# HGRN2 and stick-breaking attention block: FFN and gated embedding by Strassen's seven products on 1024-token groups

## Chip, cores and metric

The kernel runs on one core of a Trainium2 chip. The metric is the device time of one execution in microseconds; lower is better. The profile was taken of one execution of the same program.

## What is computed

One decoder layer on x of 2048 tokens x 1024 channels, float32 throughout:

```
u    = rmsnorm(x) @ w_in                      # 1024 -> 3584 columns: q, f, i, gate; q, k, v
o_hg = hgrn2(q, f, i)                         # 4 heads, 128x128 state, chunks of 64 tokens
o_hg = rmsnorm(o_hg) * silu(gate)
o_sb = rmsnorm(stick_breaking(q, k, v))       # 8 heads of 64, strictly causal
h    = x + rmsnorm(concat(o_hg, o_sb) @ w_out)
u    = rmsnorm(h)
y    = (silu(u @ w_gate) * (u @ w_up)) @ w_down     # 1024 -> 2 x 2816 -> 1024
h    = h + rmsnorm(y)
out  = h + sigmoid(h @ ple_gate) * (p @ ple_proj)   # p: 2048 x 256
```

A stick-breaking weight is a[t,s] = sigmoid(z[t,s]) times the product of (1 - sigmoid(z[t,j])) over s < j < t.

## The kernel before

The tokens are cut into four groups of 512 (`NG`, `GT`). Every float32 product is made of three TensorE matmuls on operands that are split into a rounded part hi and a rest lo: hi·hi, lo·hi, hi·lo (`mm3`, L200 to L203). A weight tile of 128x512 is loaded by SyncE into one of four buffers `wr` (L196), cast to `wh` on ScalarE (L187), and its rest `wl` is taken on GpSimd (L188). The split pairs have three buffers.

TensorE runs its instructions in program order. The order on the other engines is made by a scheduler when the program is built, and each engine then runs its own list strictly in order. `weave` (L48) writes the program order: after each slot of a main stream, such as four matmul groups of a projection, it lets side streams do a step. Four stages follow one another:

- The input projection `in_proj` of groups 0 to 3, in 56 slots each. Beside it run the recurrence `hgrn` of the group before and a share of the attention.
- An attention unit is one 128-query block against one 512-key chunk of one head: two score matmuls into `z` (L351), two sigmoids on ScalarE (`f` L359, `be` L361), a running product `pt` on VectorE by a scan (L365), the weight `a` = be·pt on VectorE (L367), four 128x128 transposes of `a` on TensorE (L378), a cast `ah` (L381), its rest `al` on VectorE (L383), and two value matmuls (L394, L395). Groups 0 to 3 have 32, 64, 96 and 128 units.
- Of the attention, the shares of groups 2 and 3 are spread at one rate over the rest of `in_proj(2)`, `in_proj(3)`, `out_proj(0)` and the FFN of group 0 (`late_share`, L728). The recurrence of group 3 also lies beside the FFN of group 0 (L773).
- Then each group has `out_proj` (192 matmuls; it ends with `post_mix`, which is norm, residual add and norm on whole 128x1024 rows, L605), transposes of h for the FFN (`make_u`) and for the embedding (`make_h2`), `ple`, and `ffn`. Streams of neighbouring groups are woven: while group g's `out_proj` runs, group g-1's transposes and embedding are stepped, so that one group's norms lie beside the other's matmuls.

The FFN of a group (`ffn`, L631) goes through 11 blocks of 256 columns. `up_block` has 8 weight tiles of 128 x (256 gate, 256 up columns) and 96 matmuls; the sigmoid (L644) and two products (L645, L646) follow, and the result is split into `hdh`, `hdl` for `down_block`, which takes four hidden tiles at a time and adds PSUM into `y` in SBUF (L666). u, h and the hidden tiles stay in SBUF. A group's FFN has 1056 + 528 matmuls, its gate 192.

Of the kernel before, what the change touches and what calls it, by code (L numbers as in the profile page):

```python
# [15 lines left out]
P = 128  # L16
# [66 lines left out]
def hybrid_block(  # L83
# [12 lines left out]
    # ---------------------------------------------------------------- scratch in DRAM  # L96
# [11 lines left out]
    hg_s = scratch("hg_s", (HH, P, GT))  # L108
    o_s = [[dram.tile([P, GT], F32, tag=f"o_s{g}_{i}", name=f"o_s{g}_{i}") for i in range(ND)] for g in range(NG)]
# [4 lines left out]
    def ctile(name, shape, dt=F32):  # L114
        return const.tile(list(shape), dt, tag=name, name=name)
# [3 lines left out]
    identb = ctile("identb", (P, P), BF16)  # L119
    make_identity(nc, identb)  # L120
    maskneg = ctile("maskneg", (P, P), BF16)
# [28 lines left out]
    masks = {h: ctile(f"mask{h}", (P, P), U8) for h in (0,) + LEVELS if h <= WIDE}  # L150
# [4 lines left out]
    # ---------------------------------------------------------------- pools  # L155
# [14 lines left out]
    wpool = ctx.enter_context(tc.tile_pool(name="wpool", bufs=1))  # L170
    side = ExitStack()
# [84 lines left out]
    # ---------------------------------------------------------------- input projection  # L256
# [68 lines left out]
    # ---------------------------------------------------------------- stick-breaking attention  # L325
    def attention():
# [18 lines left out]
        def weights_of(ch, tb):  # L345
# [21 lines left out]
            nc.vector.tensor_tensor(a[:, :n], be[:, :n], pt[:, o + 1:], op=ALU.mult)  # L367
# [59 lines left out]
    # ---------------------------------------------------------------- HGRN2  # L427
# [100 lines left out]
    # ---------------------------------------------------------------- output projection, FFN, PLE  # L528
    def tok(pool, tag):
        return [pool["p"].tile([P, D], F32, tag=tag, name=tag, bufs=TT) for _ in range(TT)]  # L530

    def gain_rows(src):
        gb = []
        for i in range(2):
            gb.append(tmp())
            nc.sync.dma_start(gb[i], src[:, i * 512:(i + 1) * 512].to_broadcast((P, 512)))
        return gb

    def scaled(dst, r, gb):
        for i in range(2):  # L540
            d = dst[:, i * 512:(i + 1) * 512]
            nc.vector.scalar_tensor_tensor(d, d, r, gb[i], op0=ALU.mult, op1=ALU.mult)
# [4 lines left out]
    def out_load(pool, g, res):  # L547
        ops = []
        acc = None
        for i in range(ND):  # L550
            raw = tmp()
            nc.sync.dma_start(raw, o_s[g][i])
            if i >= HH:
                hi, lo = operand(*pool["u"])
# [10 lines left out]
            else:  # L565
                ops.append(split(*pool["u"], raw))
        res["o"], res["oss"] = ops, acc

    def out_proj(pool, g, res):
        t0 = g * GT  # L570
        ops, acc = res["o"], res["oss"]
        r_hg, r_sb = [], []
        mix = tok(pool, "tok")
        for half in range(2):
            cs = slice(half * 512, (half + 1) * 512)
            for part in range(2):
# [24 lines left out]
                if half == 1 and part == 1:  # L601
                    post_mix(pool, g, res, mix)
                yield

    def post_mix(pool, g, res, mix):  # L605
        t0 = g * GT
        hs = tok(pool, "h")
        gb = gain_rows(attn_post_norm[0:1])
        for t in range(TT):
            nc.sync.dma_start(hs[t], x[t0 + t * P:t0 + (t + 1) * P, :])  # L610
        rs = [row_rstd(backp, mix[t], junk()) for t in range(TT)]
        for t in range(TT):
            scaled(mix[t], rs[t], gb)
            nc.vector.tensor_tensor(hs[t], hs[t], mix[t], op=ALU.add)
        rs = [row_rstd(backp, hs[t], junk()) for t in range(TT)]
        for t in range(TT):
            nc.vector.tensor_scalar(mix[t], hs[t], rs[t], None, op0=ALU.mult)
        res["h"], res["mix"] = hs, mix

    def make_u(pool, res, bank_of):  # L620
        res["u"] = []
# [213 lines left out]
```

## Time and profile before

| what | value |
|---|---|
| time, three runs | 3212.98, 3209.33, 3212.26 us; median 3212.26 |
| span of the profiled execution | 3207.7 us (the median is 4.6 above it) |
| input projections with attention and recurrence | 0 to 1011 us |
| `out_proj(0)` and the wait for its norms | 1011 to 1138 us |
| FFN of group 0 with the last attention | 1138 to 1691 us |
| groups 1 to 3, output projection to embedding | 1691 to 3208 us |
| DMA, share of 16 engines, and bytes | 41.1%, 400.70 MB |

Read a row "x896 | 1198.7, 1339" as 896 instructions, 1198.7 us busy in all, 1339 ns each on average. Where TensorE works without a gap, a matmul's own duration overlaps its neighbours', so its pace is found by dividing a stretch by its matmuls.

### The profile page before, as it was taken

The numbers are of one execution on the slowest core, as the hardware profiler recorded it, in microseconds if no ns is written. First come the engines' busy times: TensorE is split into PE (matmuls) and PEld (weight loads), VectorE is DVE, ScalarE is ACT, GpSimd is POOL, SyncE is SP. The second block draws the span as 40 slices with busy tenths as digits, with TensorE's granted clock in tenths as the row PEclk, the third lists the DMA queues.
The fourth block names the chain that finished last, engine by engine and source line by source line (L and its number), as shares of the span: only waits on it lengthen the run. The fifth ranks groups of instructions, "written<-read, shape, count | busy, mean of one in ns | idle before, by whom it ended". The sixth has DMA issues, their size and how long they took to land.

```text
span 3207.7 us, 44851 instructions
## 1 busy us (share of the span) xinstructions
PE 3124.3 (97%) x15328; PEld 2555.3 (80%) x15328; DVE 1774.9 (55%) x2492; ACT 1431.9 (45%) x2608; POOL 1494.0 (47%) x1254
## 2 busy tenths in 40 slices
PE   8999999999999799999999999999999998999999
PEld 6878878888888678888887888887888887888877
DVE  3356889888888888888866221226222226222142
ACT  4454565555456555555555332334333334332233
POOL 5444434443445423343346444556444556444453
PEclk9999999999999899999999999999999999999999
DMA  7666455545545233333343433332433333333333
GB/s 199 196 178 207 145 173 162 162 144 148 168 138 183 74 93 114 99 113 97 102 134 101 145 96 95 109 112 93 148 98 96 118 106 92 99 94 95 94 107 103
DMA packets 308420, 403.56 MB, mean 126 GB/s; under 512 B 35808, under 2 KB 177120, under 8 KB 308192
## 3 DMA queue, kind: packets, MB, share of 16 engines
q1 hardware_dynamic: 308192, 400.70, 41.1%
q8 instruction: 121, 1.98, 0.3%
q14 instruction: 107, 0.88, 0.1%
HBM read 341.85 MB, written 58.72 MB: 125 GB/s over the span
## 4 chain that ended last, share of the span: by engine, by line
PE 73%; DVE 6%; POOL 3%; issue 2%; ACT 1%; DMA 1%; SPq 0%; DVEq 0%; POOLq 0%; ACTq 0%
PE mm L201 16%; PE mm L203 15%; PE mm L202 15%; PE z L351 3%; PE tr L378 3%; PE av L201 2%; PE z L203 2%; PE z L201 2%; PE av L203 2%; PE av L202 2%; PE z L202 2%; DVE pt L365 2%; PE hg L449 2%; PE av L395 2%; POOL wl L188 1%
## 5 line engine op out<-in xcount | busy, mean ns | idle before, releaser
L188 POOL TENSOR_TENSOR wl<-wr,wh 128x512 fp32r<-128x512 f32 x896 | 1198.7, 1339 | 1415.0 <-ACT wh L187 1239.5
L187 ACT CAST wh<-wr 128x512 fp32r<-128x512 f32 x896 | 555.1, 620 | 1252.4 <-PE mm L202 422.5
L201 PE MATMUL mm<-uh,wh 128*128 128x512 f32 x1696 | 694.5, 410 | 5.3 <-DVE ea L321 4.6
L203 PE MATMUL mm<-uh,wl 128*128 128x512 f32 x1696 | 668.9, 394 | 1.0 <-POOL wl L188 0.9
L202 PE MATMUL mm<-ul,wh 128*128 128x512 f32 x1696 | 665.7, 393 | 0.0
L203 PEld LDWEIGHTS mm<-uh,wl 128*128 128x128 f32 x1696 | 318.6, 188 | 75.6 <-POOL wl L188 2.3
L201 PEld LDWEIGHTS mm<-uh,wh 128*128 128x128 f32 x1696 | 320.2, 189 | 68.9 <-DVE ea L321 5.6
L202 PEld LDWEIGHTS mm<-ul,wh 128*128 128x128 f32 x1696 | 320.3, 189 | 59.8
L365 DVE TENSOR_TENSOR_SCAN pt<-f,cy 128x513 f32<-128x513 f32 x192 | 294.5, 1534 | 69.1 <-ACT f L359 68.1
L645 DVE TENSOR_TENSOR tmp<-mm,tmp 128x512 f32<-128x512 f32 x67 | 45.4, 688 | 428.8 <-ACT tmp L644 428.6
L367 DVE TENSOR_TENSOR a<-be,pt 128x512 f32<-128x512 f32 (+2 forms) x320 | 256.7, 802 | 27.8 <-ACT ah L381 0.5
L381 ACT CAST ah<-tr 128x512 fp32r<-128x512 f32 (+1 forms) x320 | 167.1, 522 | 212.9 <-PE tr L378 209.7
L201 PE MATMUL mm<-wh,uh 128*128 128x512 f32 x616 | 255.0, 414 | 0.3 <-DVE ea L308 0.3
L202 PE MATMUL mm<-wl,uh 128*128 128x512 f32 x616 | 242.3, 393 | 8.0 <-POOL wl L188 8.0
L203 PE MATMUL mm<-wh,ul 128*128 128x512 f32 x616 | 243.0, 394 | 0.0
L365 DVE TENSOR_TENSOR_SCAN pt<-f 128x129 f32<-128x129 f32 (+3 forms) x128 | 163.4, 1277 | 124.6 <-ACT f L359 124.5
L383 DVE TENSOR_TENSOR al<-tr,ah 128x512 fp32r<-128x512 f32 (+1 forms) x320 | 192.4, 601 | 44.1 <-ACT ah L381 43.2
L359 ACT ACTIVATE f<-z 128x512 f32<-128x512 f32 (+2 forms) x320 | 170.0, 531 | 98.9 <-PE z L351 58.9
L201 PE MATMUL mm<-wh,hdh 128*128 128x512 f32 x520 | 209.0, 402 | 0.3 <-DVE tok L664 0.2
L203 PE MATMUL mm<-wh,hdl 128*128 128x512 f32 x520 | 205.3, 395 | 0.0
L202 PE MATMUL mm<-wl,hdh 128*128 128x512 f32 x520 | 205.0, 394 | 0.0
L351 PE MATMUL z<-kt,q 128*128 128x512 f32 (+3 forms) x640 | 183.7, 369 | 0.0
(252 smaller groups left out, 5157.2 us busy)
## 6 DMA issues: line engine op xcount, KB each, us to landing
wr<-in_w_gate_up_dram SPq DMA_DIRECT2D x704, 128.0 KB, 2.2
wr<-in_w_in_dram SPq DMA_DIRECT2D x224, 256.0 KB, 3.0
wr<-in_w_down_dram SPq DMA_DIRECT2D x176, 256.0 KB, 2.6
kt<-k_s SPq DMA_DIRECT2D x80, 256.0 KB, 3.0
vt<-v_s SPq DMA_DIRECT2D x80, 256.0 KB, 3.0
q<-q_s SPq DMA_DIRECT2D x128, 128.0 KB, 3.5
wr<-in_w_out_dram SPq DMA_DIRECT2D x64, 256.0 KB, 2.7
wr<-in_ple_gate_dram SPq DMA_DIRECT2D x64, 256.0 KB, 2.6
```

The source lines that it names most:

```text
L187: nc.scalar.copy(hi, src)
L188: (lo_engine or nc.gpsimd).tensor_tensor(lo, src, hi.bitcast(F32), op=ALU.subtract)
L201: nc.tensor.matmul(o, l[0], r[0], start=start, stop=False)
L202: nc.tensor.matmul(o, l[0], r[1], start=False, stop=False)
L203: nc.tensor.matmul(o, l[1], r[0], start=False, stop=stop)
L351: nc.tensor.matmul(z[:, :n], st["q"][i][:, tb * P:(tb + 1) * P], ch["k"][:, :n], start=i == 0, stop=i == 1 and not diag)
L359: nc.scalar.activation(f[:, o:GT], z[:, :n], AF.Sigmoid, scale=-0.125)
L365: nc.vector.tensor_tensor_scan(pt[:, o:][:, ::-1], fr, fr, init, op0=ALU.mult, op1=ALU.bypass)
L367: nc.vector.tensor_tensor(a[:, :n], be[:, :n], pt[:, o + 1:], op=ALU.mult)
L378: nc.tensor.transpose(tr[:, tb * P:(tb + 1) * P], ch["a"][tb][:, sb * P:(sb + 1) * P], ident)
L381: nc.scalar.copy(hi[:, lo_c:], tr[:, lo_c:])
L383: nc.vector.tensor_tensor(lo[:, lo_c:], tr[:, lo_c:], hi[:, lo_c:].bitcast(F32), op=ALU.subtract)
```

## The change

The FFN and the embedding's gate no longer work on a 512-token group but on 1024 tokens, as 2x2 blocks, by Strassen's seven products in Winograd's form: seven block products instead of eight, with sums and differences of blocks ahead of them (`t_side`, `s_side`) and sums of the results behind them (`chain`, the end of `gate_up`, `post_y`). Matmuls of 128x512 go from 10752 to 9864.

- `gate_up(grp)` goes through 11 blocks of 256 gate and 256 up columns. A block has seven products of 24 matmuls, in the order 1, 2, 6, 7, 5, 4, 3. The token side is combined and split once per group on VectorE. The weight side is combined for each block: eight sums and differences of 128x512 on VectorE (`e = nc.vector`), then 14 casts on ScalarE and 14 rests on GpSimd. The hidden tiles' own combinations are four GpSimd instructions per block, and seven tiles of each block go to DRAM.
- `down(grp)` takes two blocks at a time, loads hidden tiles back from DRAM (14 in an iteration), splits them with the rest on VectorE, combines weights on GpSimd, and adds each of 28 PSUM results into SBUF. In the last iteration the 28 results of both groups are finished row block by row block, with norm, residual and the store of h2 (`post_y`).
- `ple(grp)` combines h2 transposed on VectorE (`s_side`) and the gate's weights on GpSimd; `turn_h2` transposes h2 and sends it through DRAM.
- h, h2, u, the transposed h2, the transposed p and the hidden tiles go through DRAM scratch.
- The attention must be done before the FFN: its shares are 19 units in the rest of `in_proj(0)`, 13 + 37 beside `in_proj(1)`, 27 + 55 beside (2), 41 + 52 beside (3), and 81 units in the 48 slots of `out_proj(0)` to `(2)`; all 45 steps of `hgrn(3)` lie in the 16 slots of `out_proj(0)`. The weight product `a` goes from VectorE to GpSimd.
- Then, with nothing woven in, come `out_load(3)`, `make_u(2)`, `make_pt` of all four groups and `out_proj(3)`. `make_u(3)` is called in the first `gate_up` block after its third product, with the single bank `hg`; after it one half of the buffers is opened.

The core of the diff:

```diff
             a = att.tile([P, GT], F32, tag="a", name="a", bufs=8)
-            nc.vector.tensor_tensor(a[:, :n], be[:, :n], pt[:, o + 1:], op=ALU.mult)
+            nc.gpsimd.tensor_tensor(a[:, :n], be[:, :n], pt[:, o + 1:], op=ALU.mult)
...
+    def make_pt(g, tags):
+        for i in range(TT // 2):
+            raw = tmp().rearrange("p (t d) -> p t d", t=2)
+            nc.sync.dma_start(raw, p[r0:r0 + 2 * P, :].rearrange("(t p) d -> p t d", p=P))
+            ...
+            e = tmp()
+            nc.scalar.copy(e, b)
+            for c in range(PLE // P):
+                nc.sync.dma_start(pt_s[g][c][:, 2 * i * P:2 * (i + 1) * P], e[:, c * 2 * P:(c + 1) * 2 * P])
+    CHAIN = (1, 2, 6, 7, 5, 4, 3)
+    SLOTS = {"u": (12, 16), "w": (4, 4), "wr": (9, 0), "acc": (11, 18)}
+    def chain(prod, c, b, sides=(0, 0, 0, 1)):
+        if prod == 1:
+            c["u"] = acc(sides[0], "cu")
+            nc.scalar.copy(c["u"], b)
+        elif prod == 2:
+            c[1, 1] = acc(sides[1], "c11")
+            add(nc.vector, c[1, 1], b, c["u"])
+        elif prod == 6:
+            add(nc.vector, c["u"], b, c["u"])
+        ...
+    def gate_up(grp, hooks):
+        ts = t_side(lambda i, j, k: u_s[g0 + j][4 * i + k], ND // 2, "u", nc.vector, nc.vector)
+        for fb in range(DFF // 256):
+            for prod in CHAIN:
+                e = nc.vector
+                ...
+                elif prod == 6:
+                    a[2, 1], a[2, 2] = wload(1, 0), wload(1, 1)
+                    s1 = [acc(0, "s1") for _ in range(2)]
+                    for n in range(2):
+                        add(e, s1[n], a[2, 1][n], a[2, 2][n])
+                        sub(e, a[2, 1][n], a[1, 1][n], a[2, 1][n])
+                        sub(e, a[1, 1][n], s1[n], a[1, 1][n])
+                        sub(e, a[1, 2][n], a[1, 2][n], a[1, 1][n])
+                    w = a[1, 1]
+                else:
+                    w = {7: a[2, 1], 5: s1, 4: a[2, 2], 3: a[1, 2]}[prod]
+                ws = [pair_of(t, "w", prod, nc.gpsimd) for t in w]
+                for q in range(2):
+                    b = mm_bank()
+                    for k in range(ND // 2):
+                        mm3(b, st, tt[prod][k], k == 0, k == ND // 2 - 1)
+                    chain(prod, cs[q], b)
+                    ...
+    def down(grp):
+        for f0 in range(0, nfb, 2):
+            for prod in DOWN:
+                ...
+                hs = [pair_of(load(hid_s[grp][f0 + k, prod - 1]), "u", prod, nc.vector) for k in range(nk)]
+                ops[prod] = (hs, [pair_of(t, "w", prod, nc.gpsimd) for t in w])
+                if not last:
+                    for i in range(TT):
+                        down_product(accs, i, prod, ops[prod], nk)
+            if last:
+                for i in range(TT):
+                    for prod in DOWN:
+                        down_product(accs, i, prod, ops[prod], nk)
+                    post_y(grp, i, accs[i])
...
+    out_load(NG - 1, res[NG - 1])
+    Stream(make_u(NG - 2, res[NG - 2], ["tr", "hg"])).drain()
+    for g in range(NG):
+        make_pt(g, ["z", "av"])
+    Stream(out_proj(NG - 1, res[NG - 1])).drain()
+    gate_up(0, {(0, 6): swap})
+    down(0)
+    gate_up(1, {(3, 3): lambda: turn_h2(0), (5, 3): lambda: turn_h2(1)})
+    down(1)
+    ple(0, {7: lambda: turn_h2(2), 5: lambda: turn_h2(3)})
+    ple(1, {})
```

The list of VectorE before, in an FFN block of a later group; `mm`, `z`, `av`, `tr`, `hg` are PSUM banks, and an arrow points from the inputs to the output:

```order
L645 TENSOR_TENSOR tmp_23643<-mm_23487,tmp_23643 128x512
L645 TENSOR_TENSOR tmp_23651<-z_23488,tmp_23651 128x512
L646 TENSOR_TENSOR tmp_23643<-av_23489,tmp_23643 128x512
L646 TENSOR_TENSOR tmp_23651<-mm_23490,tmp_23651 128x512
L188 TENSOR_TENSOR hdl_23648<-tmp_23643,hdh_23647 128x512
```

The same list after, from product 2 to product 6 of a `gate_up` block (`wr` are raw weight tiles, `s1` a sum of two, `c11` and `cu` results in SBUF):

```order
L689 TENSOR_TENSOR c11_18229<-z_18216,cu_18187 128x512
L689 TENSOR_TENSOR c11_18244<-av_18231,cu_18202 128x512
L689 TENSOR_TENSOR s1_18254<-wr_18246,wr_18250 128x512
L689 TENSOR_TENSOR s1_18255<-wr_18248,wr_18252 128x512
L686 TENSOR_TENSOR wr_18246<-wr_18162,wr_18246 128x512
L686 TENSOR_TENSOR wr_18248<-wr_18164,wr_18248 128x512
L686 TENSOR_TENSOR wr_18162<-s1_18254,wr_18162 128x512
L686 TENSOR_TENSOR wr_18164<-s1_18255,wr_18164 128x512
L686 TENSOR_TENSOR wr_18204<-wr_18204,wr_18162 128x512
L686 TENSOR_TENSOR wr_18206<-wr_18206,wr_18164 128x512
L689 TENSOR_TENSOR cu_18187<-tr_18272,cu_18187 128x512
```

GpSimd after, in the same block: the first and second weight tile of product 6 are `wr_18162` and `wr_18164`; `wr_18246`, `s1_18254` and `wr_18250` are the first tiles of products 7, 5 and 4:

```order
L682 TENSOR_TENSOR wl_18265<-wr_18162,wh_18264 128x512
L682 TENSOR_TENSOR wl_18301<-wr_18246,wh_18300 128x512
L682 TENSOR_TENSOR wl_18339<-s1_18254,wh_18338 128x512
L682 TENSOR_TENSOR wl_18379<-wr_18250,wh_18378 128x512
L682 TENSOR_TENSOR wl_18269<-wr_18164,wh_18268 128x512
```

VectorE made no weights before. Now product 6's weights stand in its list behind the two evictions of product 2 (`c11`), and on GpSimd three tiles of later products stand between the two tiles of product 6.

The attention on VectorE before, with `pt`, `a`, the carry `cy` and `al` in turn:

```order
L365 SCALAR_TENSOR_TENSOR pt<-f_219 128x513
L367 TENSOR_TENSOR a<-be,pt 128x512
L371 COPY cy_10707<-pt 128x1
L383 TENSOR_TENSOR al<-tr,ah 128x512
L365 SCALAR_TENSOR_TENSOR pt<-f_217,cy_10550 128x513
L367 TENSOR_TENSOR a<-be,pt 128x512
```

GpSimd after, beside an input projection, where `qp` is the recurrence's and `wl` the projection's:

```order
L375 TENSOR_TENSOR a<-be,pt 128x512
L486 TENSOR_TENSOR qp<-qp,pd 128x128x2
L375 TENSOR_TENSOR a<-be,pt 128x512
L196 TENSOR_TENSOR wl<-wr,wh 128x512
L486 TENSOR_TENSOR qp<-qp,pd 128x64x4
L375 TENSOR_TENSOR a<-be,pt 128x512
L196 TENSOR_TENSOR wl<-wr,wh 128x512
```

The weight product has left VectorE's list and stands between the weights' rests on GpSimd.

TensorE before, at the start of the last group's output projection, behind the FFN's `down_block` of the group ahead:

```order
L201 MATMUL mm<-wh,hdh 128x512
L202 MATMUL mm<-wl,hdh 128x512
L203 MATMUL mm<-wh,hdl 128x512
L584 MATMUL hg<-ones_137,acc 128x1 x4
L201 MATMUL mm<-wh,uh 128x512
```

TensorE after, at the same place:

```order
L626 MATMUL hg<-ident,tok 128x128 x4
L640 MATMUL z<-ident,tmp 128x128 x4
L640 MATMUL av<-ident,tmp 128x128 x4
L640 MATMUL z<-ident,tmp 128x128 x4
L640 MATMUL av<-ident,tmp 128x128 x4
L640 MATMUL z<-ident,tmp 128x128 x4
L640 MATMUL av<-ident,tmp 128x128 x4
L640 MATMUL z<-ident,tmp 128x128 x4
L640 MATMUL av<-ident,tmp 128x128 x4
L583 MATMUL hg<-ones_162,acc 128x1 x4
L209 MATMUL av<-wh,uh 128x512
```

Between the matmuls of `out_proj(2)` and those of `out_proj(3)` now stand only transposes: eight rows of `tok`, the normalised h, of which the last is shown, and eight of `tmp`, which holds p. Before, FFN matmuls went right up to them.

More of the change, by code (lines that the diff above doesn't have):

```diff
@@ L741, in hybrid_block @@
         Stream(in_u(front, in_norm(front, 0), us[0], ["mm", "mm", "mm", "mm", "z", "av", "tr", "hg"])).drain()
+        before = 0
         for g in range(NG):
@@ L763, in hybrid_block @@
     h = Stream(hgrn(NG - 1))
[L764 to L773 removed]
+    out_load(0, res[0])
+    todo = before + LAG + 1
@@ new lines, in hybrid_block @@
+    for g in range(NG - 1):
+        op = Stream(out_proj(g, res[g]))
+        u = Stream(make_u(g - 1, res[g - 1], ["hg"])) if g else idle
+        n = todo // (NG - 1 - g)
+        todo -= n
+        hg_n = HG_STEPS if g == 0 else 0
+        weave(op, 6, att_part(share(n, 6, OP_SLOTS)), (h, hg_n // 2, 1))
+        weave(op, OP_SLOTS - 6, att_part(n - share(n, 6, OP_SLOTS)), (h, hg_n - hg_n // 2, 1), (u, ND if g else 0, 0))
+        out_load(g + 1, res[g + 1]) if g + 1 < NG - 1 else None
+        if g == 0:
+            h.drain()
+        op.drain()
```

498 lines of the change are left out of this document (318 added, 180 removed).

## The prediction

> **What bounds the kernel now.** First the page's busy row, then its chain, then a table of six stretches (us from to, length, then busy us and instructions of PE, PEld, DVE, ACT, POOL, and the clock).
>
> ```profile
> PE 3124.3 (97%) x15328; PEld 2555.3 (80%) x15328; DVE 1774.9 (55%) x2492; ACT 1431.9 (45%) x2608; POOL 1494.0 (47%) x1254
> ...
> PE 73%; DVE 6%; POOL 3%; issue 2%; ACT 1%; DMA 1%; SPq 0%; DVEq 0%; POOLq 0%; ACTq 0%
> ```
>
> ```profile
> 0.00:1011.00 1011.00, 979.40 (x5418) 813.13 (x5418) 734.68 (x1095) 535.10 (x1043) 458.66 (x419) 1.00 0.57 168
> 1011.00:1138.00 127.00, 106.09 (x556) 85.25 (x556) 110.50 (x171) 70.20 (x135) 50.16 (x47) 0.91 0.34 107
> 1138.00:1691.00 553.00, 548.26 (x2796) 448.74 (x2794) 453.16 (x626) 298.87 (x555) 213.05 (x167) 1.00 0.36 109
> 1691.00:2300.00 609.00, 599.99 (x2660) 484.62 (x2660) 213.48 (x261) 226.84 (x381) 327.60 (x269) 1.00 0.36 112
> 2300.00:2600.00 300.00, 300.00 (x1314) 246.83 (x1314) 71.52 (x96) 98.91 (x162) 150.24 (x116) 1.00 0.34 104
> 2600.00:3208.00 608.00, 590.52 (x2591) 476.77 (x2589) 191.51 (x245) 201.93 (x336) 294.25 (x238) 0.99 0.32 99
> ```
>
> TensorE is the bound nearly everywhere. From 2300 to 2600 us it never rests, so its pace is 300.00/1314 = 0.228 us per matmul. VectorE is loaded up to 1691 us (734.68 of 1011, 453.16 of 553) and nearly free after that (71.52 of 300). Dropping matmuls therefore pays only if TensorE stays the bound while VectorE and GpSimd get more work. For that the durations matter: of a group its mean, of a line min/median/max.
>
> ```profile
> L188 POOL TENSOR_TENSOR wl<-wr,wh 128x512 fp32r<-128x512 f32 x896 | 1198.7, 1339 | 1415.0 <-ACT wh L187 1239.5 <-PE z L351 36.8 <-PE mm L202 24.2
> L187 ACT CAST wh<-wr 128x512 fp32r<-128x512 f32 x896 | 555.1, 620 | 1252.4 <-PE mm L202 422.5 <-PE mm L203 306.2 <-PE z L202 172.9
> L188 DVE TENSOR_TENSOR hdl<-tmp,hdh 128x512 fp32r<-128x512 f32 x88 | 75.7, 891 | 3.6 <-ACT hdh L187 0.7
> ```
>
> ```profile
> L188 POOL TENSOR_TENSOR wl<-wr,wh x896: 1260/1292/2463, 17.4 to 3193.8; 128x512 fp32r<-128x512 f32 x180
> L188 DVE TENSOR_TENSOR hdl<-tmp,hdh x88: 669/679/1794, 1176.5 to 3080.5; 128x512 fp32r<-128x512 f32 x88
> L365 DVE TENSOR_TENSOR_SCAN pt<-f,cy x192: 1265/1299/2409, 336.3 to 1644.7; 128x513 f32<-128x513 f32 x192
> L367 DVE TENSOR_TENSOR a<-be,pt x320: 279/692/1821, 100.2 to 1646.1; 128x512 f32<-128x512 f32 x96, 128x128 f32<-128x128 f32 x32, 128x384 f32<-128x384 f32 x32
> L666 DVE TENSOR_TENSOR tok<-mm,tok x116: 658/692/693, 1361.5 to 3111.7; 128x512 f32<-128x512 f32 x116
> ```
>
> VectorE operations on two SBUF inputs, and GpSimd's, stretch up to about the sum of both (669 to 1794 ns; 1260 to 2463). The one that reads PSUM (L666) never exceeds 693. So those two kinds exclude one another: what counts is their **common sum**, at their shortest.
>
> The Trainium skill ("SBUF — State Buffer", section "SBUF: two separate sides") says the same of a shared port pair: it is an exclusive lock between a GpSimd operation and a VectorE operation with two SBUF inputs, held for the whole instruction. By that rule the sums below are floors, and the front cannot be bound by TensorE alone; the 669 to 1794 agrees.
>
> **The change part by part** (us of the profiled span).
>
> *Matmuls.* 10752 - 9864 = 888 fewer, 888 x 0.228 = **-202** if TensorE stays the bound.
>
> *Front: four input projections, out_proj(0) to (2), all of attention and recurrence.*
>
> ```profile
> 0.00:220.00 220.00, 201.34 (x939) 164.36 (x940) 86.62 (x127) 103.02 (x194) 99.92 (x113) 0.98 0.66 193
> ...
> 920.00:1011.00 91.00, 90.38 (x500) 74.85 (x497) 79.60 (x108) 55.34 (x107) 48.24 (x37) 1.00 0.50 155
> ```
>
> TensorE: 979.4 + 106.1, + 548.3 less FFN(0)'s 1584 x 0.228 = 361, + 2 x 192 x 0.228 = 88 for two output projections: 1361 busy. At before's pace, gaps included: 1691 - 361 + 88 = 1418. The common sum: GpSimd is busy 721.9 up to 1691, 632 with each instruction at the shortest of its shape. Less FFN(0)'s 132 weights x 1.26 = 166; plus `a`, which GpSimd does in 1.26 instead of 0.69 (median): 224 x 1.26 + some 66 for the 96 shorter ones = 348; plus out_proj(1), (2): 46 x 1.26 = 58. That makes 872. VectorE: 192 scans x 1.265 + some 107 for the 128 shorter, 350; other two-input ones some 105. Together 1327, of which 120 fall in the first 220 us, where no attention runs until late. How tightly can these lock together? Summed at their shortest over the records of 920 to 1011 they fill 82.4 of 91, 0.91, the densest stretch there is; from 370 to 1011 it is 0.80. I take 0.91: 220 + 1207/0.91 = **1545**. Bounds: 1361 (TensorE alone) and 220 + 1207/0.80 = 1729. `al` and the evictions read PSUM and lie beside it.
>
> *Ahead of out_proj(3).* Before, attention covered these norms, and yet this was seen (start, length, in brackets the idle time and its end):
>
> ```profile
> 1089.92 1.40 POOL L222 TENSOR_SCALAR rstd<-ss 128x1 f32<-128x1 f32 x1 [0.65 <-ACT junk L229]
> 1090.06 1.20 DVE L614 TENSOR_TENSOR h<-h,tok 128x1024 f32<-128x1024 f32 x1
> ...
> 1090.23 0.77 PE L394 MATMUL av<-ah,vt 128*128 128x512 f32 x1 [4.41 <-ACT junk L229]
> ```
>
> ```profile
> L542 DVE SCALAR_TENSOR_TENSOR tok<-tok,rstd,tmp 128x512 f32<-128x512 f32 x64 | 62.5, 1023 | 9.3 <-POOL rstd L224 9.0
> L617 DVE TENSOR_SCALAR tok<-h,rstd 128x1024 f32<-128x1024 f32 x16 | 23.7, 1483 | 6.7 <-POOL rstd L224 6.7
> L614 DVE TENSOR_TENSOR h<-h,tok 128x1024 f32<-128x1024 f32 x16 | 22.2, 1416 | 0.0
> L229 ACT ACTIVATE junk<-h 128x1024 bf16<-128x1024 f32 x16 | 16.9, 1056 | 25.0 <-DVE h L614 24.7 <-POOL rstd L222 0.3
> ```
>
> ```profile
> tmp<-o_s SPq DMA_DIRECT2D x32, 256.0 KB, 2.9
> ...
> tmp<-in_p_dram SPq DMA_DIRECT2D x8, 256.0 KB, 3.0
> ```
>
> `post_mix(2)`: VectorE 8 x 1.02 + 4 x 1.42 + 4 x 1.48 = 20, two rounds of squares before and between some 10: 30. `out_load(3)` with 8 and `make_pt` with 16 tiles share 3 `tmp`: loads of 2.9 and 3.0, a cast, a store of about as much, some 15 and 24; `make_u(2)` 10. All in a row 79; beside one another in part, I take 60. TensorE has 7 us of transposes there. Then 192 x 0.228 = 44: **104** (bounds 51 and 123).
>
> *gate_up, a regular block.* 168 x 0.228 = 38.3 of matmuls. Busy there: GpSimd 18 x 1.3 = 23, VectorE 30 instructions, 21; neither fills it, so only order can stall. After product 2's last matmul VectorE must do, in its list's order, the second `c11` eviction (0.69) and five sums (0.68 each); then a cast (0.62); then GpSimd five rests (1.29), since three of later products stand ahead of product 6's second tile: 11.2 us. Of product 6's 24 matmuls 17 still follow, 3.9; unstalled it would be 5.5: a **stall of 9.6**, with means for medians 10.6; I take 10. The floor is 0, if c11's eviction did not hold the sums. Queued behind those sums are product 6's own evictions, which nobody needs before product 7's end.
>
> ```profile
> 200.00:205.00 5.00, 5.00 (x16) 4.13 (x16) 1.92 (x4) 2.37 (x6) 2.97 (x5) 0.50 0.84 312
> ...
> 1092.00:1097.00 5.00, 4.23 (x15) 3.34 (x15) 4.68 (x9) 2.04 (x5) 4.92 (x2) 0.55 0.00 0
> 1097.00:1105.00 8.00, 2.83 (x22) 2.01 (x22) 7.29 (x11) 2.71 (x6) 4.12 (x7) 0.68 0.00 0
> 1105.00:1115.00 10.00, 8.30 (x40) 6.46 (x39) 9.57 (x20) 6.17 (x12) 2.23 (x3) 0.57 0.18 54
> ```
>
> After a pause of 4.41 us (above) the granted clock is 0.55 to 0.68. A 5 us stretch at 0.50 loses 2.5: the least that a row shows, and what I take per stall. So 20 blocks x (38.3 + 10 + 2.5) = 1016.
>
> The Trainium skill ("TensorE: Matmul & The Clock Gate", section "Part 1: The HAM clock gate") has half clock after an idle window of about 3.4 us, until some 3.4 us of sustained work: 1.7 per stall, 16 us less in the sum. That the drop follows such a pause agrees with 0.55 after 4.41; that it ends so soon does not, since it lasts to 1115.
>
> First blocks: VectorE splits and combines u there, 52 more instructions; 60 x 0.78 + 15 of evictions = 62, taken 64; in group 0 also `post_mix(3)` and `make_u(3)` through one bank (8 x 1.4 = 11), 88. `turn_h2` 2 x 7. Sum **1182** (bounds 877, no stall at all, and 1230).
>
> *down.* An iteration is 38.3 of matmuls; VectorE 28 x 0.69 + 14 x 0.78 = 30; common sum 22 x 1.26 + 14 x 0.67 = 37, so 41 with imperfect locking, five times. The last has 84 matmuls, 19; but VectorE does 28 evictions and 48 two-input instructions of `post_y`, 19 + 48 x 0.85 = 60, and with its ends 69; next in its list stand the sums of the following stage, so TensorE waits. 2 x (205 + 69) = **548** (bounds 421, 580).
>
> *ple.* 432 matmuls, 98.5 each. ple(0): 44 instructions of `s_side` (29 to 39) ahead of product 2's evictions, `turn_h2` 2 x 10: 150; ple(1) 127. **277** (bounds 197, 320). End: 5.
>
> Sum 1545 + 104 + 1182 + 548 + 277 + 5 = 3661, against 3207.7. The median of the runs is 4.6 above that span, so **3665**.
>
> **The rivals.**
> - *TensorE stays the bound (faster).* The weights' sums are ready before product 2 ends, as the 4 + 4 weight pairs would allow, and the front keeps before's pace: 1418 + 104 + 877 + 461 + 210 + 5 = 3075, time 3080. It decides at a stall of (3212 - 3080)/20 = 6.6 us per block, all else as here. For it: average loads of 21 and 23 in 38. Against it: the list's order, and the stretching already in the front. 0.08.
> - *The common sum does not bind the front.* `a` on GpSimd relieves VectorE, which was the dense engine (79.60 of 91); the two interleave well. Front 1418: 3538. For it: GpSimd's mean load of 872 in 1418. 0.24.
> - *The clock stays down longer.* In the three rows 1092 to 1115 it costs 5 x 0.45 + 8 x 0.32 + 10 x 0.43 = 9.1 instead of 2.5 per stall: 20 x 6.6 = +132, 3797. For it: these rows; against: few long gaps in the trace of before to judge by. 0.17.
>
> **How the numbers follow.** The forecast, with VectorE and GpSimd binding the front and a stall in each block, 0.50: 3665. The remaining 0.01 is no change. The range 3420 to 3880 takes in the second and third rival and most of the unknown costs (front -127, if at before's pace, or +184; blocks ±50); the lower end leaves out the first rival, and all upper bounds at once. A measurement of this kernel tells about 0.2% from no change. Faster by more than that 0.08, within it 0.01, slower 0.91.
>
> **What would show it.** Right: TensorE has a gap of 5 to 10 us ahead of the product 6 matmuls in every gate_up block, ended by GpSimd's `wl`; the clock falls behind it; the front ends near 1545 with VectorE and GpSimd busy and stretched; a pause of some 55 us ahead of out_proj(3); some 50 us of waiting at the end of each `down`. Wrong: blocks of 38 to 40 us, a front under 1430, or `post_y` hidden behind the next matmuls.

## The result, and the profile after

The changed kernel takes 3775.61 us (median of 4 runs, 3771.53 to 3780.8), against 3211.31 for the kernel before in the same comparison: a ratio of 1.176, 95% interval 1.1744 to 1.1777. The forecast was 3665, in a range of 3420 to 3880. The span of the profiled execution is 3769.7 us, where 3661 were summed up.

First the page of the changed kernel: busy times, two of its slice rows (40 equal slices of the span, in tenths; `PEclk` is the granted TensorE clock), and the chain. The last line is the clock row of the kernel before.

```profile
PE 3115.8 (83%) x14440; PEld 2482.3 (66%) x14440; DVE 2150.4 (57%) x3042; ACT 1520.9 (40%) x2852; POOL 2069.5 (55%) x1756
...
PE   8999999999987766666888889966878888992668
...
PEclk9999999999998887877988889987878889996789
...
PE 49%; DVE 14%; POOL 11%; issue 11%; DMA 10%; ACT 4%; SPq 1%; POOLq 0%; DVEq 0%; ACTq 0%
```

```profile
PEclk9999999999999899999999999999999999999999
```

TensorE has 888 instructions fewer (15328 to 14440), and yet its busy time hardly falls (3124.3 to 3115.8): the same matmuls run at a lower clock, as the clock rows show, with 8 and 7 in many slices from the thirteenth on where there was 9 before. Its share of the chain falls from 73% to 49%; VectorE, GpSimd, DMA and the time in which no wait is seen (`issue`, 2% to 11%) grow. What TensorE waited for stands in the list of its waits (total us, times, longest):

```profile
PE tr L209 <- ACT wh L681: 111.7, 22, 12.5
PE mm L209 <- ACT wh L681: 109.7, 3, 65.1
PE hg L583 <- POOL acc L564: 67.4, 2, 35.5
PE tr L211 <- POOL wl L682: 65.4, 43, 2.9
PE z L209 <- ACT wh L681: 33.0, 4, 28.0
```

The first and the fourth row are the 22 gate_up blocks: once per block a wait for a cast weight, twice for a rest. The others stand at places that come once or twice: the ends of `down` and of `ple`, and the starts of `out_proj(1)` and `(2)`.

The stages, from the first matmul of each to the first of the next (worked out from the records of the trace), against the terms of the prediction:

| stage | predicted | measured |
|---|---|---|
| front, to the last matmul of out_proj(2) | 1545 | 1564.5 |
| wait ahead of out_proj(3), and out_proj(3) | 60 + 44 | 83.1 + 45.7 |
| gate_up, two groups | 1182 | 1196 |
| of it a regular block (18 of them, mean) | 50.8 | 50.6 |
| down, two groups | 548 | 574 |
| ple and the end | 282 | 306 |

The differences add up to the 109 us between 3661 and 3769.7.

### The profile page after: what moved, and what is told of

Same layout as the page of the kernel before. It is cut to its first block, busy times and chain, and to the rows that moved or that the text cites. A ratio compares the mean times of both kernels' runs of the same rounds, so it can differ in the third digit from the quotient of the medians.

```text
span 3769.7 us, 45073 instructions
## 1 busy us (share of the span) xinstructions
PE 3115.8 (83%) x14440; PEld 2482.3 (66%) x14440; DVE 2150.4 (57%) x3042; ACT 1520.9 (40%) x2852; POOL 2069.5 (55%) x1756
## 4 chain that ended last, share of the span: by engine, by line
PE 49%; DVE 14%; POOL 11%; issue 11%; DMA 10%; ACT 4%; SPq 1%; POOLq 0%; DVEq 0%; ACTq 0%
PE mm L209 9%; PE mm L210 9%; PE mm L211 9%; POOL wl L682 5%; DMA wr<-hid_s 5%; PE tr L386 3%; PE z L359 3%; DVE pt L373 2%; PE hg L457 2%; DVE y L689 2%; POOL hs L686 2%; DVE ul L682 2%; PE av L403 2%; POOL wr L686 1%; PE tr L211 1%
## 5 line engine op out<-in xcount | busy, mean ns | idle before, releaser
L209 PE MATMUL mm<-uh,wh 128*128 128x512 f32 x1344 | 560.2, 417 | 52.3 <-ACT wh L681 44.6
L375 POOL TENSOR_TENSOR a<-be,pt 128x512 f32<-128x512 f32 (+2 forms) x320 | 315.9, 988 | 315.0 <-DVE pt L373 222.7
L209 PE MATMUL mm<-wh,uh 128*128 128x512 f32 x1008 | 422.8, 419 | 76.1 <-ACT wh L681 65.1
L210 PE MATMUL mm<-wl,uh 128*128 128x512 f32 x1008 | 404.2, 401 | 6.3 <-POOL wl L682 6.0
L211 PE MATMUL mm<-wh,ul 128*128 128x512 f32 x1008 | 403.5, 400 | 0.0
L682 DVE TENSOR_TENSOR ul<-wr,uh 128x512 fp32r<-128x512 f32 x274 | 238.1, 883 | 221.2 <-ACT uh L681 220.4
L681 ACT CAST uh<-wr 128x512 fp32r<-128x512 f32 x274 | 166.5, 619 | 369.7 <-DMA wr<-hid_s 246.0
L209 PEld LDWEIGHTS mm<-wh,uh 128*128 128x128 f32 x1008 | 194.9, 193 | 128.0 <-ACT wh L681 67.9
L210 PEld LDWEIGHTS mm<-wl,uh 128*128 128x128 f32 x1008 | 194.9, 193 | 45.4 <-POOL wl L682 9.1
L211 PEld LDWEIGHTS mm<-wh,ul 128*128 128x128 f32 x1008 | 193.9, 192 | 45.4
```

The costliest lines, as they stand in the source:

```text
L209: nc.tensor.matmul(o, l[0], r[0], start=start, stop=False)
L210: nc.tensor.matmul(o, l[0], r[1], start=False, stop=False)
L211: nc.tensor.matmul(o, l[1], r[0], start=False, stop=stop)
L375: nc.gpsimd.tensor_tensor(a[:, :n], be[:, :n], pt[:, o + 1:], op=ALU.mult)
L681: nc.scalar.copy(hi, src)
L682: lo_engine.tensor_tensor(lo, src, hi.bitcast(F32), op=ALU.subtract)
```

## The experiments

Each experiment but the last is one run. The changed kernel's own four runs lie 9 us apart, so a gain of 10 us or less is not read from the time alone but from the stages in the trace.

**The stall in a gate_up block.** A timeline of one block of the changed kernel (start, length, in brackets the idle time before and what ended it), from the last matmul of product 2 to the second weight tile of product 6:

```profile
1884.36 0.39 PE L211 MATMUL av<-uh,wl 128*128 128x512 f32 x1
1884.88 0.69 DVE L689 TENSOR_TENSOR c<-av,cu 128x512 f32<-128x512 f32 x1 [1.97 <-PE av L211]
1885.49 1.28 DVE L689 TENSOR_TENSOR s<-wr 128x512 f32<-128x512 f32 x2
1886.69 1.29 DVE L686 TENSOR_TENSOR wr<-wr 128x512 f32<-128x512 f32 x2
1887.89 1.29 DVE L686 TENSOR_TENSOR wr<-s,wr 128x512 f32<-128x512 f32 x2
1888.62 1.14 ACT L681 CAST wh<-wr 128x512 fp32r<-128x512 f32 x2 [8.71 <-DVE wr L686]
1889.29 0.80 PE L209 MATMUL tr<-uh,wh 128*128 128x512 f32 x1 [4.54 <-ACT wh L681]
1889.31 3.47 POOL L682 TENSOR_TENSOR wl<-wr,wh 128x512 fp32r<-128x512 f32 x2 [7.37 <-ACT wh L681]
...
1892.71 1.31 POOL L682 TENSOR_TENSOR wl<-s,wh 128x512 fp32r<-128x512 f32 x1
1893.96 3.73 POOL L682 TENSOR_TENSOR wl<-wr,wh 128x512 fp32r<-128x512 f32 x3
...
1896.52 0.80 PE L211 MATMUL tr<-uh,wl 128*128 128x512 f32 x1 [2.00 <-POOL wl L682]
```

It is the chain of the order: VectorE evicts `c` only when TensorE has finished product 2, then come the sums, the cast, and the rests on GpSimd. Nothing there is busy for long; each waits for the one before. The windows of the same block (from, to, length, busy of PE, PEld, DVE, ACT, POOL, clock) show what the clock makes of it:

```profile
1884.00:1889.00 5.00, 0.75 (x4) 0.28 (x2) 4.12 (x7) 0.39 (x1) 0.00 (x0) 0.85 0.00 0
1889.00:1895.00 6.00, 4.15 (x8) 2.34 (x8) 1.39 (x3) 3.88 (x8) 5.69 (x4) 0.50 0.25 74
1895.00:1900.00 5.00, 3.48 (x8) 2.84 (x9) 0.69 (x1) 0.00 (x0) 5.00 (x5) 0.50 0.59 157
1900.00:1903.00 3.00, 3.00 (x12) 2.39 (x12) 0.39 (x1) 1.20 (x2) 1.47 (x2) 0.82 0.37 120
1903.00:1924.00 21.00, 21.00 (x93) 16.97 (x92) 9.82 (x15) 4.21 (x8) 6.52 (x5) 1.00 0.16 51
```

Two kernels took the two causes apart. The first writes the loads and sums ahead of product 1, and with them the pairs of products 1 and 2 (`a[1, 2]` is overwritten by the sums):

```diff
                 if prod == 1:
-                    a[1, 1] = wload(0, 0)
+                    a[1, 1], a[1, 2] = wload(0, 0), wload(0, 1)
+                    a[2, 1], a[2, 2] = wload(1, 0), wload(1, 1)
                     w = a[1, 1]
-                elif prod == 2:
-                    a[1, 2] = wload(0, 1)
-                    w = a[1, 2]
-                elif prod == 6:
-                    a[2, 1], a[2, 2] = wload(1, 0), wload(1, 1)
+                    ws1 = [pair_of(t, "w", 1, nc.gpsimd) for t in a[1, 1]]
+                    ws2 = [pair_of(t, "w", 2, nc.gpsimd) for t in a[1, 2]]
                     s1 = [acc(0, "s1") for _ in range(2)]
                     for n in range(2):
...
+                elif prod == 2:
+                    w = a[1, 2]
+                elif prod == 6:
                     w = a[1, 1]
...
```

> The loads and the eight VectorE sums of a gate_up block are written ahead of product 1's matmuls instead of behind product 2, so in VectorE's list they come in the block before. Theory (the list's order makes the stall: sums behind the c11 evictions, then the rests): the pause ahead of product 6 goes, a regular block takes 38 to 40 us instead of 50.8, 20 blocks give -220 to -250, time 3525 to 3555, and the clock in these blocks returns to 1.00. Rival (GpSimd's or the weight tiles' throughput sets the block): blocks stay at 45 us or more, time above 3650.

It (e1) took 3549.42 us, 226 less than the changed kernel's median. A regular block takes 38.9 us instead of 50.6, and TensorE does not pause in it. A window of ten blocks' length (its last 6 us lie in `down`):

```profile
1794.00:2181.00 387.00, 387.00 (x1682) 315.43 (x1681) 233.29 (x303) 122.76 (x207) 257.51 (x188) 1.00 0.34 108
```

VectorE, GpSimd and the weight loads keep up with a TensorE that never rests, so their throughput was not the limit. The loads moved along with the sums, but in the timeline above the sums follow `c` without a gap, so they were not waiting for weights. The second kernel leaves the sums where they are and moves only the two rests of product 6:

```diff
-                ws = [pair_of(t, "w", prod, nc.gpsimd) for t in w]
+                ws = [pair_of(t, "w", prod, nc.vector if prod == 6 else nc.gpsimd) for t in w]
```

> Of the changed kernel only the two rests wl of product 6 go to VectorE, behind the sums; the sums stay where they are. Theory (both lists add to the stall): the wait for the second weight tile behind three rests of later products goes, 3 x 1.29 us, while the wait for c11 and the sums stays: 4 to 6 us less per block, time 3655 to 3695. Rival (only VectorE's list counts): within 20 us of 3775. Rival (only GpSimd's list counts): blocks near 40 us, time near 3550.

e2: 3699.15 us, 76 less; a block takes 47.3 us, 3.3 less, a little short of the expected 4 to 6. Pauses per block went from 7.6 to 5.2 us. The wait for the cast stays at 4.5 us; the two waits for a rest become one of 0.5 to 1.0. So both lists add to the stall, and VectorE's is the larger part.

**What sets the front.** The theory on record was the common sum of two-input VectorE operations and GpSimd.

```diff
-            nc.gpsimd.tensor_tensor(a[:, :n], be[:, :n], pt[:, o + 1:], op=ALU.mult)
+            nc.vector.tensor_tensor(a[:, :n], be[:, :n], pt[:, o + 1:], op=ALU.mult)
```

> The weight product a goes back to VectorE; nothing else. Theory (VectorE's two-input operations and GpSimd's exclude one another, their common sum sets the front): the sum falls by 320 x about 0.5 us, input projections 1 to 3 go from 918 to 830 to 870 us, where TensorE is the bound again, time 3690 to 3730. Rival (VectorE is the dense engine of the front, and a on GpSimd relieves it): VectorE gains some 220 us, the three stages take 950 us or more, time 3800 or more.

e3: 3803.27 us, 28 more. The rival's time came, but not its stage: the three input projections took 940 us instead of 918, where the theory had at most 870 and the rival at least 950. Their window and what TensorE waited for longest in it, in the changed kernel, then in this one:

```profile
195.00:1113.00 918.00, 885.43 (x5070) 734.69 (x5070) 701.79 (x1000) 535.50 (x1062) 607.30 (x546) 0.99 0.53 156
...
PE av L403 <- DVE al L391: 12.9, 14, 2.2
```

```profile
195.00:1135.00 940.00, 892.46 (x5072) 731.89 (x5072) 801.67 (x1225) 536.39 (x1063) 381.88 (x321) 1.00 0.51 153
...
PE av L403 <- DVE al L391: 41.4, 51, 2.4
```

GpSimd lost 225 us and VectorE gained only 100 (`a` takes 171 us there, while its other operations on two SBUF inputs went from 438 to 391), and still the stretch became longer. With each operation at the shortest of its shape, the common sum fell from some 830 of 918 to some 744 of 940: it cannot be what set the 918. TensorE can: it is busy in 885 of 918, and in 892 of 940 now. Of the 33 and 48 us left, 12.9 and 41.4 are waits for VectorE's `al`. The theory falls here, and the second rival of the prediction (the common sum does not bind) holds for the input projections; that VectorE is the denser engine shows in the sign and in the waits for `al`.

**The stretch of out_proj(0) to (2).** From 1113 to 1565 us no engine is full, and the clock is down:

```profile
1113.00:1565.00 452.00, 324.57 (x1676) 266.15 (x1674) 273.62 (x388) 212.22 (x400) 220.13 (x217) 0.83 0.34 109
1565.00:1648.00 83.00, 19.66 (x73) 13.80 (x74) 35.90 (x43) 34.43 (x59) 31.27 (x28) 0.51 0.73 247
```

Two of its pauses, 31.9 and 35.5 us, stand before the first matmul of out_proj(1) and (2), which needs `out_load`'s sum of squares (third row of the waits above). The first attempt put attention there:

```diff
         hg_n = HG_STEPS if g == 0 else 0
+        cover = 12 if g else 0
+        n -= cover
+        for _ in range(cover):
+            att_stream.step(2)
```

> In out_proj(1) and (2) 12 of the attention units are put ahead of the first instruction of the output projection, the 128x1 matmuls that wait for out_load; the number of units stays the same. Theory (the pauses of 31.9 and 35.5 us stand only because no other TensorE work is in program order before the waiting instruction): they fall under 15 us each, time 3715 to 3745. Rival (the attention of these stages is slow by itself, or waits for the same engines): what is gained there is lost later, time within 15 us of 3775.

e4: 3766.6 us, 9 less. The pauses went (none over 5 us is left there), but the stretch to the last matmul of out_proj(2) became only 12 us shorter, for 67 us of pauses: attention without projection matmuls between its units is slow. A window in the first of the two places, and what TensorE waited for from 1300 to 1500 us:

```profile
1316.00:1355.00 39.00, 26.48 (x80) 17.90 (x81) 33.05 (x42) 23.85 (x48) 24.61 (x25) 0.65 0.66 220
```

```profile
PE av L403 <- DVE al L391: 20.6, 12, 4.7
PE av L402 <- ACT ah L389: 7.0, 9, 2.7
```

The twelve units lie between the last matmul of out_proj(0) at 1321.7 us and the first of out_proj(1) at 1370.0: 48 us, 4 us each. VectorE is busy for 33.05 of the 39 us shown, 15.3 of them with `post_mix`. But when `post_mix` is done, at 1338.0, it still takes 3.5 us from one `al` to the next. The rival holds. The other kernels build on the one with early sums (3549.42 us). One went at the cause of the pause, the buffers and SyncE's list:

```diff
-        gb = gain_rows(attn_post_norm[0:1], tmp)
+        gb = gain
...
-            nc.sync.dma_start(hs[t], x[g * GT + t * P:g * GT + (t + 1) * P, :])
+            nc.scalar.dma_start(hs[t], x[g * GT + t * P:g * GT + (t + 1) * P, :])
...
-            nc.sync.dma_start(h_s[g][t * P:(t + 1) * P, :], hs[t])
+            nc.scalar.dma_start(h_s[g][t * P:(t + 1) * P, :], hs[t])
...
+    gain = gain_rows(attn_post_norm[0:1], lambda: backp.tile([P, 512], F32, tag="gb", name="gb", bufs=2))
```

(To make room, `UB` went from 10 to 9.)

> On top of the kernel with early sums (3549): the gain rows of post_mix are loaded once into buffers of their own, and its loads of x and stores of h are issued by ScalarE, so that out_load's loads come early in SyncE's list and find free tmp buffers. Theory (the pauses of 36 and 32 us at the starts of out_proj(1) and (2), and part of that ahead of (3), are out_load waiting behind post_mix for buffers and in the list): 10 to 18 us less at each, time 3500 to 3525. Rival (the attention units around it set the pace, as where they were used as cover): within 10 us of 3549.

g3: 3538.90 us, 10.5 less, but not there: the pauses are still 30.1 and 35.4 us, and 6.8 us of the gain lie in the stage of out_proj(0), 245.7 to 238.9. SyncE's list now has the eight loads one behind another, yet issuing them takes 19.29 us. The rows of squares (`junk`) use the same three buffers; the third load is issued when the last row is done, the others as buffers come free:

```profile
1323.19 19.29 SPq L552 DMA_DIRECT2D tmp<-o_s  x8
...
1334.59 1.14 ACT L195 CAST uh<-tmp 128x512 fp32r<-128x512 f32 x2 [4.37 <-DMA h_s<-h]
```

The second row shows a wait that the edit itself made. The first two tiles had landed at 1325.81 and 1328.42 us, some 10 us earlier than in the changed kernel (1338.01 and 1338.69), but ScalarE casts them at 1334.59: the loads of x that it now issues stand ahead in its list, and the last of them waits for a store of h to land. So g3 does not tell whether the buffers set the pause. `post_mix` and then `out_load` pass through them in turn; what the pause would be with more buffers, or with those loads on another queue, was not tried. The last one here shifted attention between the three stages:

```diff
-        n = todo // (NG - 1 - g)
+        n = todo // (NG - 1 - g) if g else todo // 2
```

> On top of the kernel with early sums (3549): of the 81 attention units beside out_proj(0) to (2), 40 instead of 27 go to out_proj(0) and 20 to 21 to each of the others. Theory (out_proj(0) is set by the serial chain of the recurrence, 45 steps in 16 slots, so attention there is free): its stage stays within 10 us of 246 and the other two fall by 30 to 42 in all, time 3507 to 3520. Rival (the attention units themselves set the pace of these stages): out_proj(0) grows by as much, time within 12 us of 3549.

f7: 3544.33 us, 5 less. out_proj(0) grew by 16.5 us for 13 units more, the other two fell by 13 and 10. The theory's 10 us in out_proj(0) were passed, and the time is the rival's, though the exchange was not quite even: in out_proj(0) a unit costs 1.3 us, elsewhere some 1.8.

**The wait ahead of out_proj(3).** The transposes of p moved to in_proj(0):

```diff
-            h = Stream(hgrn(g - 1)) if g else idle
+            h = Stream(hgrn(g - 1)) if g else Stream(make_pt(i, ["z", "av"]) for i in range(NG))
...
-            weave(main, KQV - HG_START, att_part(before - before * HG_START // KQV), (h, hg_a, 1))
+            weave(main, KQV - HG_START, att_part(before - before * HG_START // KQV), (h, hg_a if g else NG, 1))
...
-    for g in range(NG):
-        make_pt(g, ["z", "av"])
```

> On top of the kernel with early sums (3549): the transposes of p of all four groups (make_pt) move from ahead of out_proj(3) into in_proj(0). Theory (the wait ahead of out_proj(3) is a chain through the three tmp buffers, of which make_pt is the last 31 us): 25 to 35 us less, time 3515 to 3525. Rival (out_load(3) and make_u(2) end no earlier, make_pt lay beside them): within 10 us of 3549.

f5: 3549.49 us: no change, and yet both halves moved. The wait ahead of out_proj(3) fell by 29.3 us, as the theory had it, and in_proj(0) grew by 31.0. There TensorE stood before the second tile of each group until its load had landed (four waits, 21.9 us, the longest 11.2), and the clock in that stage fell from 1.00 to 0.94. A second kernel loads each tile one step ahead, and its steps lie further apart:

```diff
...
+        ahead = p_load(*todo[0])
+        yield
+        for n, (g, i) in enumerate(todo):
+            raw = ahead
+            if n + 1 < len(todo):
+                ahead = p_load(*todo[n + 1])
+            yield
...
```

> On top of the kernel with early sums (3549): make_pt in in_proj(0) as in f5, but each tile of p is loaded one step ahead of its transposes, and the steps lie further apart. Theory (in f5 in_proj(0) grew by 31 us because TensorE waited in order for each load of 3 us): in_proj(0) grows by less than 10 us, the 29 us ahead of out_proj(3) stay gained, time 3520 to 3532. Rival (the wait is for the copy and the store through the three tmp buffers): in_proj(0) again above 195 us, time above 3540.

g2: 3527.13 us, 22 less: in_proj(0) grew by 8.6 us only, the waits for p are gone, and the 29.3 stayed.

**The ends of down.** VectorE or the common sum?

```diff
                 hr = load(h_s[g][r0:r0 + P, j * 512:(j + 1) * 512])
-                add(nc.vector, y, y, hr)
+                add(nc.gpsimd, y, y, hr)
```

> On top of the kernel with early sums (3549): the last sum of post_y, y + h, 32 instructions per group, goes from VectorE to GpSimd. Theory (at the ends of down the two-input operations of VectorE and all of GpSimd's exclude one another, so the common sum counts): each move adds 1.26 - 0.67 = 0.6 us, 5 to 20 us more in all, time 3554 to 3570. Rival (VectorE's list alone is the bound there): 32 x 0.7 us less, time near 3527.

f6: 3555.90 us, 6.5 more. (The sums are 16 in each group, 32 in both, so that the theory's price is at most 32 x 0.6 = 19.) The last iterations of the two groups took 65.9 and 91.1 us instead of 60.4 and 84.6 (59.6 to 60.4 and 84.6 to 86.3 in the other kernels with early sums, g1 aside), with less work on VectorE. The second of them with early sums, and then with the sum on GpSimd:

```profile
3155.00:3240.00 85.00, 20.51 (x87) 15.73 (x85) 79.06 (x115) 26.47 (x58) 34.31 (x39) 0.64 0.59 199
```

```profile
3159.00:3250.00 91.00, 20.06 (x86) 15.38 (x84) 74.44 (x99) 25.66 (x58) 55.61 (x55) 0.63 0.56 186
...
DVE y L924 <- POOL rstd L232: 6.7, 2, 4.8
```

VectorE is no longer full (74.44 of 91), GpSimd neither, and it is slower: the rival falls. Two readings are left. With each operation at its shortest the common sum was 84 of 85 us before the sums moved and is 94 of 91 with them: it is full here, as it was not in the front, though it passes the window, so it is no strict floor. But the last row, VectorE's wait for GpSimd's `rstd`, was not there with early sums; it is 6.7 us in each of the two iterations, about what they grew by. On GpSimd `rstd` now stands between the sums that were moved there. f6 does not tell these two apart.

**ple.** Two attempts on its waits of 64 and 30 us. In the first the stores of the output are issued by ScalarE:

```diff
-                    nc.sync.dma_start(out[r0:r0 + P, j * 512:(j + 1) * 512], y)
+                    nc.scalar.dma_start(out[r0:r0 + P, j * 512:(j + 1) * 512], y)
```

> On top of the kernel with early sums (3549): the stores of out in ple are issued by ScalarE instead of SyncE. Theory (SyncE's list is in order, a store that waits for its sum holds back the loads behind it, and TensorE waits 28 us in ple(0) for them): ple falls by 20 to 35 us, time 3515 to 3530. Rival (the wait is for the operands' own chain or for VectorE): within 8 us of 3549.

f8: 3549.51 us: nothing. The timeline of the changed kernel ahead of ple(1) suggests why: the first weights of the gate are not loaded behind a store but behind all loads of the token side.

```profile
3628.34 17.86 SPq L671 DMA_DIRECT2D wr<-h2t_s  x14
...
3647.08 3.34 SPq L671 DMA_DIRECT2D wr<-in_ple_gate_dram  x5
...
3650.91 1.62 POOL L682 TENSOR_TENSOR wl<-wr,wh 128x512 fp32r<-128x512 f32 x1 [57.71 <-ACT wh L681]
```

So the second put the first product's weights ahead of the token side:

```diff
-        ss = s_side(lambda i, j, k: h2t_s[g0 + i][4 * j + k], ND // 2, "u", nc.vector, nc.vector)
...
         ws = t_side(blk, ND // 2, "w", nc.gpsimd, nc.gpsimd)
+        tt = next(ws)
+        ss = s_side(lambda i, j, k: h2t_s[g0 + i][4 * j + k], ND // 2, "u", nc.vector, nc.vector)
```

> On top of the kernel with early sums (3549): in ple the first product's weights are loaded and split ahead of the token side, whose 28 loads and 44 VectorE instructions stand ahead of them in the lists. Theory (TensorE's waits of 64 us before ple(0) and 30 us before ple(1) are for the first weight tile, whose load is issued behind all token loads): together 20 to 50 us less, time 3500 to 3530. Rival (product 1's token pairs, behind post_y on VectorE, come as late): within 8 us of 3549.

g1: 3546.19 us, 3 less. What TensorE waited for (the second row lies in ple(1), the others in ple(0)):

```profile
PE mm L209 <- ACT uh L681: 39.7, 2, 39.4
PE mm L209 <- ACT wh L681: 16.1, 1, 16.1
PE tr L209 <- ACT wh L681: 13.5, 1, 13.5
```

The named waits did shrink, 64 to 39 us and 30 to 3; but from their first matmul on the two stages grew by 22 and 25. The wait of 39 is now for a token operand (`uh`), and those of 13.5 and 16.1 us stand ahead of product 2, whose weights are loaded behind the token side, as product 1's were. The wait moved on to the next weights in the same list.

**Together.** e1, g2, g3 and f7 in one kernel:

> Early sums, p early with loads ahead (g2), loads of post_mix apart (g3) and more attention in out_proj(0) (f7), together. If the gains lie in different pauses they add: 3549 - 22 - 11 - 5 = 3511, and the ratio to the kernel before is about 1.095, so still slower. If g3 and f7 gain in the same stage (out_proj(0)), 3516 to 3520. In neither case does it reach the kernel before; what then stands between them is the end of the two down stages, the first gate_up blocks, ple and the output projections of groups 0 to 2.

3518.42 us, ratio 1.0962 to the kernel before, interval 1.0944 to 1.098. The parts gave 31 of the 38 us that they had each shown, as expected if g3 and f7 gain in the same place: out_proj(0) took 259.8 us, where f7 alone had 262.2. No version that was run beats the kernel before.

## Why the prediction came out as it did

- *Matmuls.* -202 us was right as a count, and the full pace returns where nothing stalls (387 us for ten blocks, 1.00).
- *gate_up* was right in mechanism and place, shown by e1 (the whole stall goes) and e2 (a part). That 50.8 was predicted and 50.6 measured is partly luck, since its two terms were off against one another. The pauses are 7.6 us per block instead of 10, and the lower clock costs 50.6 - 38.7 - 7.6 = 4.3 instead of 2.5. That the slower matmuls of product 6 fill part of the wait for the second tile was left out. The sign that was named, one gap of 5 to 10 us ended by GpSimd's `wl`, came as three: 4.5 us ended by ScalarE's cast, then 1.1 and 2.0 for `wl`. Two blocks with `turn_h2` took 13 to 15 us more, where 7 was put.
- *Front.* 1545 against 1564.5 looks right and is not. The step that failed is "VectorE and GpSimd binding the front", a common sum at 0.91. e3 showed that the input projections are set by TensorE, with waits for VectorE's `al`. That the sum counted there and divided by 0.91 gives 912 us, where 918 were measured, is luck. In out_proj(0) to (2) it gives 363 (331 at the shortest), and 452 were measured, with TensorE's 1676 instructions busy for 325 even at a clock of 0.83. The sum itself was too large: the trace has some 1280 up to 1565 us instead of 1327, mostly because `a` takes 1.09 us on GpSimd at 128x512 and not 1.26. Nor did the sums as floors show that TensorE could not bind the front: 1327 is less than the prediction's own 1361 for TensorE. The two pauses of 67 us together were not on the list at all: the prediction looked for `post_mix` and `out_load` only where nothing is woven in, and took the attention as cover ahead of out_proj(1) and (2). In program order it stands behind the instruction that waits. What sets the rest of this stretch stays open: e4, g3 and f7 shortened it by 6 to 12 us only.
- *Ahead of out_proj(3).* The pieces, all in a row, had been put at 79 and were taken as 60; measured 83.1. They stand in a row: f5 took make_pt out, and the wait fell by 29, close to the 24 worked out for it, so it had not lain beside the rest. That the three `tmp` buffers are the reason was not tried.
- *down.* Regular iterations took 41 to 45, 42.8 on average, against 41; the last ones 59.9 and 86.0 against 69 each. VectorE is full in these (79.06 of 85), and f6 showed that its load alone does not decide. The second is longer because ple(0)'s token side follows in the same list, which was counted under ple: with the weights ahead of it (g1) this iteration took 60.4 to ple's first matmul.
- *ple.* 306 with the end, against 282: the token side's loads, ahead of the weights in SyncE's list, were missing. g1 showed that it is this list, not the first weight alone, that TensorE waits for.
- The rival of a clock that stays down longer (9.1 us per stall) did not come: 4.3. The rows from 1092 to 1115 us that it was worked out from hold more than one pause (TensorE busy in 2.83 of 8 us), so their 9.1 was not the price of one stall. The rival on the faster side needed a stall under 6.6 us per block; e1 made it 0, and 3549 instead of 3080 came, because its other condition, a front at before's pace with everything else unstalled, failed.

Where the 202 us of saved matmuls went, and 562 more: 226 to the blocks' stalls (e1). The other places stand only as differences to the bounds that the prediction had worked out for a TensorE without stalls, and together with the 226 they come to 825, 61 more than there is to explain, so these bounds lie too low in part: 231 for the front with the wait and out_proj(3) (1693.3 against 1418 + 44), 153 for down (574 against 421), 109 for ple (306 against 197), 106 for the first gate_up blocks (80.5 and 75.5 against 38.3) and `turn_h2`. The kernel before had almost none of these outside its front, where one group's norms and transposes lay beside another group's matmuls (TensorE busy in 599.99 of 609 and 590.52 of 608 us).

## What to carry to other kernels

Fewer matmuls pay only where the work that prepares their operands stands early enough in every engine's list: e1 moved no work to another engine and took none away, and it returned 226 us. Ask of each wait not only what ends it but what is queued behind that: three kernels (e4, f5, g1) removed or shortened the named wait and moved the time elsewhere. And ask what else an edit puts into a list: g3's loads and f6's sums each made a new wait on the engine that took them. A loop that handles one group alone seems to need another group's work beside it, or its norms, loads and transposes become the path; g2 is the one run here that bears this out, with 22 us.

## What was not expected of the hardware

- After a pause of 4.5 us the clock stays at 0.50 from 1889 to 1900 us, 11 us, in which TensorE was busy for 7.6 of 11 with short pauses between; with uninterrupted matmuls behind it, 0.82 from 1900 to 1903 and 1.00 after that. The Trainium skill ("TensorE: Matmul & The Clock Gate", section "Part 1: The HAM clock gate") has half clock until some 3.4 us of sustained work; the pauses of 1.08 and 2.00 us within those 11 us fit that reading, though no run here separates them from the first. Nor do equal pauses cost the same: in the second block, with pauses of 4.51, 1.07 and 2.02 us, the clock was 0.50 from 1789 to 1795 us and 1.00 from 1796 to 1810.
- VectorE's other operations on two SBUF inputs took 391 us instead of 438 when `a` left GpSimd (e3), so the two engines do slow one another, but at a common sum of 0.90 over 918 us that did not set the pace. Whether it does at 0.99 of 85 us, at the end of `down`, f6 leaves open.
